# Low parts of 21 weight tiles: subtracted on GpSimd before, added up by an accumulating DMA after

## Chip, core and metric

The kernel runs on one core of a Trainium2 chip. The metric is device time in microseconds (us) of one execution. Five engines run their own instruction queues: TensorE (PE, with its weight loads PEld), VectorE (DVE), ScalarE (ACT), GpSimd (POOL) and SyncE (SP). Sixteen DMA engines move data for the queues of SP, ACT and POOL.

## What is computed

One decoder layer over 512 tokens of width 1024, in float32:

```python
h = rmsnorm(x, norm_mix[l]) * (1 + sc1) + sh1
z = h @ w_in[l]
z_attn, z_rwkv, z_conv, z_gate = split_cols(z, (ATTN_COLS, RWKV_COLS, CONV_COLS, GATE_COLS))
o_attn = dsa_attention(z_attn, positions, rel_bias)
o_rwkv = rwkv7_mix(z_rwkv, ...)
o_conv = c_b * causal_dwconv(c_c * c_x, sc_conv_w[l])
merged = sum(gates[:, :, i] * (o @ w_branch[l, i]) for i, o in enumerate((o_attn, o_rwkv, o_conv)))
x = x + g1 * (merged @ w_o[l])
x = x + g2 * conv_glu_ffn(h, ffn_w_up[l], ffn_conv_w[l], ffn_w_down[l])
```

(The second `h` is normed again, and a final norm follows.) The RWKV mix is a recurrence over time, done here in eight chunks of 64 tokens.

## The kernel before

Every large product is made of three passes, so that it has nearly float32 accuracy: each operand is split into a high part (rounded to the type fp32r) and a low part (what the rounding left), and PE adds high times high, high times low and low times high in one PSUM bank.

The projection by `w_in` goes in columns of 128 output channels. `z_col` makes one: `w_in` calls `weights`, which loads 128x1024 float32 values (512 KB, tile `wraw`, four buffers) by SP's queue, makes the high part `whi` on ACT and the low part `wlo = wraw - whi` on POOL (three buffers each); `mm_t` then issues 24 matmuls of 512 columns (eight rows k, three passes, lines L177, L178 and L179; the third reads `wlo`). The first five RWKV columns have their own buffers (`xraw`, `xhi`, `xlo`; the argument `own`) in the opening stage. The change touches the 21 columns that follow: nine of RWKV and twelve of the short convolution. After them come 18 attention columns or blocks, and later gates, branches, output projection and FFN.

The framework orders each engine's queue itself, from priorities: the weight work stands at a high priority, and the matmuls of the columns are woven between the RWKV steps on PE. An engine takes its queue strictly in order. The stages that matter here, in us of the profiled span:

- about 75 to 190: four RWKV passes (loop over `p`), each with a long row of small DVE steps (`rsqt`, `km`, `kn`, `AR`, `BK`, `r`: L243 to L505) that feed small matmuls on PE (`L486` transposes `km`, `L507` sums `r`, `L528` makes `LM`), and POOL's share (`BK` L548, `LG` L539).
- about 190 to 228: a serial substitution of 31 steps on DVE (`st` L569, `sub` L571), while PE does convolution columns.
- its result goes out to memory and back (`blk`, `Dm`); then PE multiplies by it (`L588`), and the eight chunks follow, to 310; then the RWKV tail.
- about 340 to 405: bias masks on DVE (`mk` L721) and their matmuls on PE, with attention columns and the modulation weights (`ada_w`).
- about 405 to 440: values, query and key loads, the rest of a run of `ada_w` loads.

POOL's queue also issues small loads: `g_up` (L413) and `up` (L447, L448), which the first RWKV pass multiplies by at L464.

Of the kernel before, what the change touches and what calls it, by code (L numbers as in the profile page):

```python
# [15 lines left out]
AF = mybir.ActivationFunctionType  # L16
ALU = mybir.AluOpType
# [42 lines left out]
def hybrid_block(ctx, tc, ins, out, consts, dbg=None, stop=99):  # L60
    nc = tc.nc
    PE, ACT, DVE, POOL, SP = nc.tensor, nc.scalar, nc.vector, nc.gpsimd, nc.sync
# [7 lines left out]
    def dram(name, offset, ap):  # L70
        t = ins[name]
        return bass.AP(tensor=t.tensor, offset=t.offset + offset, ap=ap)
# [10 lines left out]
    def right_pool(name):  # L83
        es = ExitStack()
        es.pool = es.enter_context(tc.tile_pool(name=name, bufs=1, side="right", reuse_waits="tile"))
        return es

    def left_pool(name):
        es = ctx.enter_context(ExitStack())
        es.pool = es.enter_context(tc.tile_pool(name=name, bufs=1, reuse_waits="tile"))  # L90
        return es
# [41 lines left out]
        return colv[tag][:, r + i:r + i + n]  # L133


    lo_engine = [POOL]

    wp = left_pool("wp")
    n_raw = 4
# [1 line left out]
    def load_raw(shape, srcs, own=None):  # L141
        if own is None:
            raw = wp.pool.tile(shape, F32, name="wraw", tag="wraw", bufs=n_raw)
        else:
            raw = own[0].tile(shape, F32, name="xraw", tag="xraw", bufs=own[1])
        for dst, ap in srcs:
            SP.dma_start(dst(raw), ap)
        return raw

    def weights(name, base, ld, k0, kt, cols, own=None, raw_own=None):  # L150


        wid = sum(n for _, n in cols)
        srcs, o = [], 0
        for c, n in cols:
            srcs.append(((lambda r, o=o, n=n: r[:, :, o:o + n]),
                         dram(name, base + k0 * 128 * ld + c, [[ld, 128], [128 * ld, kt], [1, n]])))
            o += n
        raw = load_raw([128, kt, wid], srcs, raw_own)
        pool, tag, bufs = (wp.pool, "w", 3) if own is None else (own[0], "x", own[1])  # L160
        with tc.high_priority(offset=4000):
            hi = pool.tile([128, kt, wid], F32R, name=tag + "hi", tag=tag + "hi", bufs=bufs)
            ACT.activation(hi, raw, AF.Copy)  # L163
            lo = pool.tile([128, kt, wid], F32R, name=tag + "lo", tag=tag + "lo", bufs=bufs)
            lo_engine[0].tensor_tensor(lo, raw, hi, op=ALU.subtract)  # L165
        return hi, lo

    def w_in(c0, n=128, k0=0, kt=8):
        return weights("w_in", 0, C_GATE + 3 * D, k0, kt, [(c0, n)])
# [148 lines left out]
    def first_columns(step):  # L318
        if step < len(first_cols):
            w_first[step] = weights("w_in", 0, C_GATE + 3 * D, 0, 8, [(C_RWKV + first_cols[step] * 128, 128)],  # L320
                                    own=(start.pool, len(first_cols)), raw_own=(start.pool, 8))
        for k in range(step + 1):
            for j in range(min(step + 1, len(first_cols))):
                if max(k, j) != step:
                    continue
                (hi, lo), ps = w_first[j], z_first[first_cols[j]]
                PE.matmul(ps, hi[:, k, :], hT[0][:, k, :], start=k == 0, stop=False)
                PE.matmul(ps, hi[:, k, :], hT[1][:, k, :], start=False, stop=False)
                PE.matmul(ps, lo[:, k, :], hT[0][:, k, :], start=False, stop=k == 7)
# [127 lines left out]
    for p in range(4):  # L457
# [52 lines left out]
        for w0 in range(0, 9, 4):  # L510
# [7 lines left out]
            lo = 1 if w0 == 0 else 0  # L518
# [184 lines left out]
    tap("o_conv", o_cv)  # L703


    adp = left_pool("adp")
    bi = right_pool("bi")

# [197 lines left out]
    def branch(i, o, first, last):  # L906
        for m2 in range(4):
            gate = []
            for m in range(2):
                ps = z_col(C_GATE + i * D + (m2 * 2 + m) * 128)  # L910
                sg = wk()
                if first:
                    ACT.activation(sg, ps, AF.Sigmoid)
                else:
                    ACT.activation(sg, ps, AF.Tanh, scale=0.5)
                for _ in range(4):
                    next(ada, None)
                gate.append(sg)
            for m in range(2):
                mm = m2 * 2 + m  # L920
                w = weights("w_branch", i * MIX * D, D, 0, 4, [(mm * 128, 128)])
                ps = mm_bank()
                mm_t(ps, w, o)
                dst = merged[:, mm, :]
                if first:
                    ACT.activation(dst, ps, AF.Copy, scale=2.0)
                    POOL.tensor_tensor(dst, dst, gate[m], op=ALU.mult)
                    continue
                DVE.scalar_tensor_tensor(gate[m], gate[m], 1.0, ps, op0=ALU.add, op1=ALU.mult)
                DVE.tensor_tensor(dst, dst, gate[m], op=ALU.add)  # L930
                if last:
                    ACT.activation(mg_hl[0][:, mm, :], dst, AF.Copy, scale=0.5)
                    DVE.scalar_tensor_tensor(mg_hl[1][:, mm, :], dst, 0.5, mg_hl[0][:, mm, :], op0=ALU.mult, op1=ALU.subtract)
# [387 lines left out]
```

## Time and profile before

| | us |
|---|---|
| median of 3 runs | 1178.88 |
| lowest to highest of these | 1178.0 to 1181.76 |
| the profiled execution | 1178.41 |
| its span on the core | 1176.7 |
| PE busy | 1068.0 (91%) |
| DVE busy | 744.2 (63%) |
| ACT busy | 447.3 (38%) |
| POOL busy | 366.2 (31%) |

Shares are means over stages of different limits; PE's busy time is that of pipelined matmuls, each of which is listed longer than the step from one to the next. The kernel's stages are read one by one below.

### The profile page before, as it was taken

The numbers are of one execution on the slowest core, as the hardware profiler recorded it, in microseconds if no ns is written. First come the engines' busy times: TensorE is split into PE (matmuls) and PEld (weight loads), VectorE is DVE, ScalarE is ACT, GpSimd is POOL, SyncE is SP. The second block draws the span as 40 slices with busy tenths as digits, with TensorE's granted clock in tenths as the row PEclk, the third lists the DMA queues.
The fourth block names the chain that finished last, engine by engine and source line by source line (L and its number), as shares of the span: only waits on it lengthen the run. The fifth ranks groups of instructions, "written<-read, shape, count | busy, mean of one in ns | idle before, by whom it ended". The sixth has DMA issues, their size and how long they took to land.

```text
span 1176.7 us, 17739 instructions
## 1 busy us (share of the span) xinstructions
PE 1068.0 (91%) x6822; PEld 878.9 (75%) x6822; DVE 744.2 (63%) x1331; ACT 447.3 (38%) x765; POOL 366.2 (31%) x258
## 2 busy tenths in 40 slices
PE   4889899799989989977889999997999999899996
PEld 4667677577757877765667888886988888888885
DVE  5888776833578929996445343488766676762326
ACT  4253333132334424323445333465544344442313
POOL 4233233322212344546565200015345446100001
PEclk9899999999989989989899999999999999999999
DMA  9641123231345993469975533622322332562201
GB/s 328 188 108 41 42 58 94 80 75 37 117 126 145 288 259 117 122 187 240 219 194 139 154 86 103 178 88 74 108 78 67 108 103 77 164 215 104 90 1 72
DMA packets 191649, 149.31 MB, mean 127 GB/s; under 512 B 18211, under 2 KB 167101, under 8 KB 191565
## 3 DMA queue, kind: packets, MB, share of 16 engines
q1 hardware_dynamic: 162605, 122.57, 36.2%
q0 software_dynamic: 5904, 11.08, 4.5%
q10 hardware_dynamic: 23056, 14.53, 4.2%
q8 instruction: 53, 0.87, 0.3%
q14 instruction: 31, 0.25, 0.1%
HBM read 129.53 MB, written 18.63 MB: 126 GB/s over the span
## 4 chain that ended last, share of the span: by engine, by line
PE 51%; DVE 23%; DMA 11%; issue 8%; POOL 4%; ACT 3%; SPq 0%; ACTq 0%; POOLq 0%; DVEq 0%
PE mm L179 6%; PE mm L177 6%; PE mm L178 6%; DMA xraw<-in_ada_w 3%; DMA wraw<-in_ffn_w_up 3%; DMA bt<-bias_d 2%; DVE acc L217 2%; PE sd L1245 2%; PE sd L1246 2%; PE sd L1247 2%; PE sd L177 2%; PE sd L178 2%; PE sd L179 2%; DVE sub L571 2%; DVE wlo L1012 1%
## 5 line engine op out<-in xcount | busy, mean ns | idle before, releaser
L165 POOL TENSOR_TENSOR wlo<-wraw,whi 128x1024 fp32r<-128x1024 f32 (+1 forms) x70 | 157.5, 2253 | 274.7 <-ACT whi L163 217.2
L177 PE MATMUL mm<-h_hi,whi 128*128 128x512 f32 (+2 forms) x496 | 199.9, 404 | 1.1 <-DVE o_cv L702 0.7
L178 PE MATMUL mm<-h_lo,whi 128*128 128x512 f32 (+2 forms) x496 | 199.3, 402 | 1.6 <-DVE h_lo L1071 1.5
L179 PE MATMUL mm<-h_hi,wlo 128*128 128x512 f32 (+2 forms) x496 | 199.6, 403 | 0.0
L163 ACT ACTIVATE whi<-wraw 128x1024 fp32r<-128x1024 f32 (+1 forms) x86 | 80.1, 934 | 224.2 <-PE mm L178 94.0
L178 PEld LDWEIGHTS mm<-h_lo,whi 128*128 128x128 f32 (+1 forms) x496 | 94.5, 191 | 21.5 <-DVE h_lo L1071 2.0
L177 PEld LDWEIGHTS mm<-h_hi,whi 128*128 128x128 f32 (+1 forms) x496 | 94.3, 191 | 20.7 <-issue 1.4
L179 PEld LDWEIGHTS mm<-h_hi,wlo 128*128 128x128 f32 (+1 forms) x496 | 94.7, 191 | 19.4 <-issue 0.2
L1012 DVE TENSOR_TENSOR wlo<-wraw,whi 128x1024 fp32r<-128x1024 f32 x46 | 64.9, 1410 | 61.7 <-ACT whi L1011 60.9
L1011 ACT ACTIVATE whi<-wraw 128x1024 fp32r<-128x1024 f32 x46 | 48.6, 1057 | 78.9 <-DMA wraw<-in_ffn_w_up 28.7
L217 DVE SCALAR_TENSOR_TENSOR acc<-xraw,ccol,acc 128x512 f32<-128x512 f32 x56 | 59.4, 1060 | 29.4 <-DMA xraw<-in_ada_w 28.8
L1029 POOL TENSOR_TENSOR fS<-wraw 128x512 f32<-128x512 f32 x13 | 19.5, 1500 | 182.0 <-DVE wk L986 108.0
L1042 PE MATMUL sd<-mg_hi,shi 128*128 128x256 f32 x156 | 44.9, 288 | 8.6 <-DVE p L1185 8.6
L1012 DVE TENSOR_TENSOR slo<-wraw,shi 128x1024 fp32r<-128x1024 f32 x28 | 35.5, 1266 | 21.2 <-ACT shi L1011 21.0
L1288 POOL TENSOR_TENSOR f<-f 128x512 f32<-128x512 f32 x4 | 5.7, 1414 | 135.0 <-ACT wk L988 135.0
L721 DVE TENSOR_SCALAR mk<-posq,thr 128x512 f16<-128x512 f32 (+3 forms) x128 | 45.6, 428 | 3.2 <-PE sd L727 3.2
L177 PE MATMUL mm<-o,whi 128*128 128x512 f32 x96 | 39.9, 415 | 6.2 <-DVE modc L203 6.2
L1044 PE MATMUL sd<-mg_hi,slo 128*128 128x256 f32 x156 | 44.3, 284 | 0.0
L178 PE MATMUL sd<-h_lo,whi 128*128 128x512 f32 x112 | 44.3, 395 | 0.0
L177 PE MATMUL sd<-h_hi,whi 128*128 128x512 f32 x112 | 44.2, 395 | 0.0
L179 PE MATMUL sd<-h_hi,wlo 128*128 128x512 f32 x112 | 44.2, 395 | 0.0
L1043 PE MATMUL sd<-mg_lo,shi 128*128 128x256 f32 x156 | 44.2, 283 | 0.0
(522 smaller groups left out, 2776.4 us busy)
## 6 DMA issues: line engine op xcount, KB each, us to landing
wraw<-in_w_in SPq DMA_DIRECT2D x61, 512.0 KB, 4.2
xraw<-in_ada_w SPq DMA_DIRECT2D x96, 256.0 KB, 3.9
wraw<-in_ffn_w_up SPq DMA_DIRECT2D x44, 512.0 KB, 4.3
wraw<-in_ffn_w_down SPq DMA_DIRECT2D x22, 512.0 KB, 3.4
wraw<-in_w_branch SPq DMA_DIRECT2D x24, 256.0 KB, 3.6
bias_d<-stage ACTq DMA_DIRECT2D x10, 512.0 KB, 4.9
wraw<-in_w_o SPq DMA_DIRECT2D x8, 512.0 KB, 3.8
z_att<-wk ACTq DMA_DIRECT2D x12, 256.0 KB, 2.2
```

The lines of the kernel that those rows point to most:

```text
L163: ACT.activation(hi, raw, AF.Copy)
L165: lo_engine[0].tensor_tensor(lo, raw, hi, op=ALU.subtract)
L177: PE.matmul(ps, hi[:, k, :], ahi[:, k0 + k, :], start=start and k == 0, stop=False)
L178: PE.matmul(ps, hi[:, k, :], alo[:, k0 + k, :], start=False, stop=False)
L179: PE.matmul(ps, lo[:, k, :], ahi[:, k0 + k, :], start=False, stop=stop and k == kt - 1)
L217: DVE.scalar_tensor_tensor(acc, raw, ck, acc, op0=ALU.mult, op1=ALU.add)
L721: DVE.tensor_scalar(m_[:, :n], posq[:, b * 128:], thr[:, b, gg:gg + 1], None, op0=ALU.is_ge)
L1011: ACT.activation(hi, src, AF.Copy)
L1012: DVE.tensor_tensor(lo, src, hi, op=ALU.subtract)
L1042: PE.matmul(ps, w[0][:, k], b[0][:, k], start=first and k == 0, stop=False, skip_group_check=True)
L1043: PE.matmul(ps, w[0][:, k], b[1][:, k], start=False, stop=False, skip_group_check=True)
L1044: PE.matmul(ps, w[1][:, k], b[0][:, k], start=False, stop=k == 3, skip_group_check=True)
```

## The change

For the 21 columns after the opening stage and before the attention columns, ACT writes the negated high part into `wlo`, and a DMA on POOL's queue adds `wraw` to it in place. POOL no longer subtracts there. All other weight tiles are made as before. The title given to the change also names 128-row query-key passes; these (`two_pass`) stand in the kernel before already, and the diff does not touch them.

```diff
-    lo_engine = [POOL]
+    lo_engine, lo_by_dma = [POOL], [True]
...
             hi = pool.tile([128, kt, wid], F32R, name=tag + "hi", tag=tag + "hi", bufs=bufs)
             ACT.activation(hi, raw, AF.Copy)
             lo = pool.tile([128, kt, wid], F32R, name=tag + "lo", tag=tag + "lo", bufs=bufs)
-            lo_engine[0].tensor_tensor(lo, raw, hi, op=ALU.subtract)
+            if lo_by_dma[0] and own is None:
+                ACT.activation(lo, hi, AF.Copy, scale=-1.0)
+                POOL.dma_start(lo, raw, accum_op=ALU.add)
+            else:
+                lo_engine[0].tensor_tensor(lo, raw, hi, op=ALU.subtract)
...
     tap("o_conv", o_cv)
 
 
+    lo_by_dma[0] = False
     adp = left_pool("adp")
```

POOL's queue from the opening stage into the first two RWKV passes, before:

```order
L165 TENSOR_TENSOR xlo<-xraw,xhi 128x1024 x5
L165 TENSOR_TENSOR wlo<-wraw,whi 128x1024 x3
L413 DMA g_up<-in_rwkv_g_up 128x512
L447 DMA up<-in_rwkv_w_up 64x512
L448 DMA up<-in_rwkv_a_up 64x512
L165 TENSOR_TENSOR wlo<-wraw,whi 128x1024 x2
L548 TENSOR_TENSOR BK<-BK,pc 128x512
L539 COPY LG<-LM 32x256 x2
```

And the same place after (line numbers are four or so higher):

```order
L169 TENSOR_TENSOR xlo<-xraw,xhi 128x1024 x5
L167 DMA wlo<-wraw 128x1024 x3
L417 DMA g_up<-in_rwkv_g_up 128x512
L451 DMA up<-in_rwkv_w_up 64x512
L452 DMA up<-in_rwkv_a_up 64x512
L167 DMA wlo<-wraw 128x1024 x2
L552 TENSOR_TENSOR BK<-BK,pc 128x512
L543 COPY LG<-LM 32x256 x2
```

Each subtraction became a DMA issue at the same place, and the loads of `g_up` and `up` stand behind three of them.

ACT's queue at the first RWKV pass, before:

```order
L473 ACTIVATE iP<-cs 128x512
L163 ACTIVATE whi<-wraw 128x1024
L423 ACTIVATE r<-mm,rcol 128x512
L423 ACTIVATE k<-mm,rcol 128x512
L472 ACTIVATE P<-cs 128x512
L163 ACTIVATE whi<-wraw 128x1024
L473 ACTIVATE iP<-cs 128x512
```

And after:

```order
L477 ACTIVATE iP<-cs 128x512
L163 ACTIVATE whi<-wraw 128x1024
L427 ACTIVATE r<-mm,rcol 128x512
L166 ACTIVATE wlo<-whi 128x1024
L427 ACTIVATE k<-mm,rcol 128x512
L476 ACTIVATE P<-cs 128x512
L163 ACTIVATE whi<-wraw 128x1024
L166 ACTIVATE wlo<-whi 128x1024
L477 ACTIVATE iP<-cs 128x512
```

The new copies stand right behind the high parts or one instruction later, ahead of `k` and `iP`, which feed DVE.

PE's queue where the substitution's result is used (62 of 64 small matmuls by `Dm`), before:

```order
L179 MATMUL mm<-h_hi,wlo 128x512
L177 MATMUL mm<-h_hi,whi 128x512
L588 MATMUL sd<-Dm,LG 32x32 x62
L178 MATMUL mm<-h_lo,whi 128x512
L179 MATMUL mm<-h_hi,wlo 128x512
```

And after:

```order
L181 MATMUL mm<-h_hi,whi 128x512
L182 MATMUL mm<-h_lo,whi 128x512
L592 MATMUL sd<-Dm,LG 32x32 x62
L183 MATMUL mm<-h_hi,wlo 128x512
L181 MATMUL mm<-h_hi,whi 128x512
```

Counted from the start, 520 column matmuls stand ahead of these 62 before and 533 after; ahead of the two by `Dm` that come first it is 488 and 492, and ahead of the RWKV tail's transposes (`MV`, L669) 695 and 710. So the chunks and the tail stand later in PE's order by 13 to 15 column matmuls, and as many fewer are left for the mask stage.

## Rows read from the trace of the kernel before

**Rows 1.** Tile `wlo` from 187 to 252: count, ns min/median/max, first and last start.

```profile
L165 POOL TENSOR_TENSOR wlo<-wraw,whi x10: 2352/2406/2623, 187.8 to 251.2; 128x1024 fp32r<-128x1024 f32 x10
```

**Rows 2.** Windows: stretch, length; PE, PEld, DVE, ACT, POOL busy us; clock, DMA share, GB/s.

```profile
75.00:190.00 115.00, 101.75 (x633) 78.84 (x634) 83.65 (x168) 42.11 (x74) 31.95 (x22) 0.96 0.23 57
190.00:228.00 38.00, 37.26 (x161) 29.66 (x160) 34.20 (x62) 7.03 (x8) 12.69 (x6) 1.00 0.32 86
228.00:250.00 22.00, 14.68 (x172) 11.38 (x170) 7.66 (x14) 4.83 (x6) 8.82 (x4) 0.84 0.52 120
...
340.00:405.00 65.00, 62.66 (x808) 46.60 (x807) 60.43 (x151) 28.39 (x57) 19.76 (x8) 0.97 0.68 202
405.00:440.00 35.00, 29.36 (x214) 27.86 (x213) 10.87 (x12) 7.26 (x11) 14.87 (x15) 0.90 1.06 283
```

**Rows 3.** What PE waited for from 75 to 250: us in total, times, longest.

```profile
PE sd L588 <- DMA Dm<-blk: 7.3, 1, 7.3
PE sd L486 <- DVE km L483: 5.9, 4, 3.5
PE sd L507 <- DVE r L505: 5.8, 4, 2.5
PE sd L464 <- DMA up<-in_rwkv_w_up: 1.0, 1, 1.0
```

**Rows 4.** Timeline of POOL: start us, duration us, instruction, idle before.

```profile
69.69 0.55 POOL L447 DMA_DIRECT2D up<-in_rwkv_w_up  x1
...
82.18 2.34 POOL L165 TENSOR_TENSOR wlo<-wraw,whi 128x1024 fp32r<-128x1024 f32 x1 [11.41 <-ACT whi L163]
...
198.93 2.47 POOL L165 TENSOR_TENSOR wlo<-wraw,whi 128x1024 fp32r<-128x1024 f32 x1 [3.15 <-ACT whi L163]
```

**Rows 5.** Timeline of DVE: the same instructions beside POOL's subtraction and away from it.

```profile
69.91 0.17 DVE L391 TENSOR_TENSOR rbd<-rbd,rb 128x8 f32<-128x8 f32 x1
...
82.19 2.36 DVE L245 SCALAR_TENSOR_TENSOR rsqy<-rsqt,rsqy 128x8 f32<-128x8 f32 x1
...
84.98 0.17 DVE L245 SCALAR_TENSOR_TENSOR rsqy<-rsqt,rsqy 128x8 f32<-128x8 f32 x1
...
198.48 0.30 DVE L571 TENSOR_TENSOR sub<-sub,st 128x135 f32<-128x135 f32 x1
...
199.18 2.40 DVE L571 TENSOR_TENSOR sub<-sub,st 128x156 f32<-128x156 f32 x1
...
220.76 2.89 DVE L691 SCALAR_TENSOR_TENSOR wk<-wk,cw 128x510 f32<-128x510 f32 x1
```

**Rows 6.** Timeline of PE: first use of a `wlo`, and around the wait for `Dm`.

```profile
70.94 0.40 PE L179 MATMUL mm<-h_hi,wlo 128*128 128x512 f32 x1
...
236.09 0.39 PE L588 MATMUL sd<-Dm,LG 32*32 32x32 f32 x4 [7.32 <-DMA Dm<-blk]
...
237.43 0.63 PE L178 MATMUL mm<-h_lo,whi 128*128 128x512 f32 x1
237.85 0.63 PE L179 MATMUL mm<-h_hi,wlo 128*128 128x512 f32 x1
```

**Rows 7.** Timeline of ACT: the high parts of the first three columns, and of two convolution columns.

```profile
59.62 2.94 ACT L163 ACTIVATE whi<-wraw 128x1024 fp32r<-128x1024 f32 x3
...
192.20 1.06 ACT L163 ACTIVATE whi<-wraw 128x1024 fp32r<-128x1024 f32 x1 [3.08 <-PE mm L178]
...
197.79 1.06 ACT L163 ACTIVATE whi<-wraw 128x1024 fp32r<-128x1024 f32 x1 [3.90 <-PE mm L178]
```

**Rows 8.** DMA issues: transfer, queue, count, KB each, median us from issue to landing.

```profile
x<-in_x POOLq DMA_DIRECT2D x4, 512.0 KB, 5.7
...
qi<-z_att POOLq DMA_DIRECT2D x8, 192.0 KB, 10.5
...
g_up<-in_rwkv_g_up POOLq DMA_DIRECT2D x1, 256.0 KB, 5.1
...
up<-in_rwkv_w_up POOLq DMA_DIRECT2D x1, 128.0 KB, 6.0
```

## The prediction, made before the changed kernel ran

> **What bounds the kernel now.** I read the windows first, since the mean of 91% hides the stages. From 75 to 190 us, the four RWKV passes, PE is busy 101.75 of 115 us, so 13.25 us idle; from 190 to 228 it is busy 37.26 of 38; from 228 to 250 only 14.68 of 22, at a granted clock of 0.84 [rows 2]. The reader is to see that PE has time to give back in two places alone here, and both lie in the stretch that the change touches. Next I asked who ends these waits. In the passes it is DVE: 5.9 us before the transposes of `km` and 5.8 us before the sums of `r`; at 236 it is one wait of 7.3 us for `Dm`, the result of DVE's substitution [rows 3].
>
> Then I read why DVE is late. A step of 128x8 elements takes 0.17 us at 84.98, and 2.36 us at 82.19; POOL's `wlo` began at 82.18 and ran 2.34 us [rows 4, 5]. In the substitution a step takes 0.30 us at 198.48 and the next size 2.40 us at 199.18, where POOL's `wlo` had begun at 198.93 and ran 2.47 us [rows 4, 5]. So a DVE instruction with two inputs in SBUF stands still for as long as POOL subtracts. I count seven such DVE rows from 82 to 175 (the first is that at 82.19), with an excess over the undisturbed row of 13.8 us in sum, and five from 193 to 221 (the last is that at 220.76), with 10.5 us. That POOL takes 2.4 us for one [rows 1] is not in itself what hurts: it is busy 31.95 of the passes' 115 us [rows 2].
>
> **Removed: 21 subtractions on POOL.** Their own time is on no path. What returns is DVE's 13.8 + 10.5 us, and PE gets of it only what it waited.
>
> In the passes PE waited 11.7 us for `km` and `r` [rows 3]. PE's order weaves column matmuls between the steps, and some of the lost DVE time is already covered by them, so I take two thirds, 8 us. Bounds: 4 us (half of the locks cost PE nothing) and 11.7.
>
> In the substitution all five locks lie on DVE's one chain, with DVE busy 34.2 of 38 us [rows 2], so `Dm` comes some 10 us sooner. PE stands ready at 228.8 (236.09 less 7.32 [rows 6]) and has four column matmuls more ahead of its first `Dm` matmul in the new order, which is under 1 us. The wait of 7.3 us goes. Behind it the column matmuls and the chunks are PE's own work in its own order, so I see no wait that takes its place. After the wait PE ran at half clock: matmuls follow each other at 0.42 us (237.43 to 237.85 [rows 6]), where a column of 24 takes 5.59 us (192.20 to 197.79, the cadence of ACT's `whi`, which PE releases [rows 7]), 0.233 us each. Nine matmuls ran so, up to 240.4: 9 x 0.19 = 1.7 us. Gap: 9.0 us. Bounds: 7.3 to 9.0, if PE is fed.
>
> **Added: 21 copies on ACT.** The nearest row is `whi`, the same shape, 1.06 us [rows 7]. Nine fall in the passes, where ACT is busy 42.11 of 115 us [rows 2], and some stand ahead of `k` and `iP`, which DVE waits for. If each met the path with that share of 0.37 and half its length, it would be 9 x 1.06 x 0.37 / 2 = 1.8 us; I take 2. Bounds: 0 and 5 (half of 9.5). In the substitution ACT is busy 7.03 of 38 us: nothing.
>
> **Added: 21 accumulating DMAs.** No row shows one. Call the time from issue to landing T. POOL issues a software-queue DMA in 0.55 us [rows 4], a fifth of the subtraction, so `BK` and `LG` behind it are not later. T's nearest rows are the loads of that queue: 5.7 us for 512 KB in 128 rows, 5.1 for 256 KB [rows 8]. The added DMA reads two streams of 512 KB and writes one. 256 KB more cost 0.6 us there, so I add 1.2 us for the second stream and take T = 6.9. Bounds: 5.7, and 10.5 from `qi` [rows 8], which ran while the DMA engines were fully taken (the last window of [rows 2]).
>
> What hides T: three buffers. A buffer is free when its column ends; two other columns, 2 x 5.6 us, and two matmuls, 0.5 us, pass before PE needs the new low part: 11.7 us. High part and copy take 2 x 1.14 us (a `whi` starts at 197.79 and its `wlo` at 198.93 [rows 4, 7]). So T up to 9.4 us costs nothing where columns follow each other without a break, which is from 187 to 251: nine columns of the changed kind (the tenth of [rows 1] is the first attention column). Above that every microsecond of T costs one for each three columns, 3.0 us per us. At T = 10.5 that is 3.3 us. In the passes a column comes about every 12 us (nine from 82 to 187), and T may be near 20. The four `wraw` buffers are held longer too, but four columns without a break last 22.4 us, so they bind later than the three.
>
> The Trainium skill speaks against such a queue. Its page "SBUF — State Buffer", section "SBUF: two separate sides", warns that a DMA issued from GpSimd needs its descriptors written through a port that it shares with VectorE, so that a VectorE instruction of the two-port kind starves it. The rows speak against a large effect: `up` was issued in 0.55 us while DVE worked, and a DVE step with two inputs beside that issue took its usual 0.17 us [rows 4, 5]. By the rule T grows by one such DVE step at most, some 0.5 us (an estimate); at my T the sum stays, at the upper bound it is 1.5 us worse.
>
> **Moved.** At the start, `g_up` and `up` stand behind three DMAs instead of three subtractions. The third `wlo` can be issued when ACT has done six copies, 59.62 + 6 x 0.98 = 65.5 (three took 2.94 [rows 7]), so `up` goes at about 66.8 instead of 69.69, and lands by 73 to 76 with three transfers ahead of it; PE waited 1.0 us for it [rows 3]. Gain 1.0, bounds +1.0 and -4 (T of 10.5, one behind the other). The first low part is issued at about 61.8 and needed at 70.94 [rows 6], which allows T = 9.1. On PE the RWKV tail comes 15 column matmuls later, 3.5 us. The mask stage behind it is nearly full on DVE, 60.43 of 65 us, as well as on PE, 62.66 [rows 2], so that DVE cannot make up for a late start: 3.5 us lost. Bounds: 0 and 5.
>
> **Sum.** 8.0 - 2.0 + 9.0 + 1.0 - 3.5 = 12.5 us. The profiled execution took 1178.41 us (its span 1176.7 and 1.7 around it), 0.5 us under the median of the runs, so 1178.4 - 12.5 = 1165.9 us. With all the best bounds it is 11.7 + 9.0 + 1.0 = 21.7, 1156.7 us; with the worst 4 - 5 + 7.3 - 4 - 5 - 3.3 = -6.0, 1184.4 us.
>
> **Rivals.**
> The transfer is slow, and the kernel slower. If T is above 9.4 us, PE waits on `wlo` in the nine dense columns; at T = 9.4 + 12.5/3.0 = 13.6 the gain is gone, and from 14.8 the kernel is slower by more than 0.3%. At T = 16 it is 12.5 - 19.8 = -7.3, 1185.7 us. For it: nothing in the trace shows an addition in the DMA path. Against it: no software-queue load took above 10.5 us, and that among full DMA engines; between 190 and 228 the DMA share is 0.32.
>
> The gain is given back from 340 to 440. The masks are DVE work beside POOL's subtractions that remain, and from 405 to 440 the DMA engines are full (share 1.06 [rows 2]); a new order of loads there could wait longer. Price: the 5.6 us that PE stands idle in that last window once more, plus up to 7 us of new locks on the mask row, which together take it all: 1178 us. For it: both stages are tight. Against: nothing in them starts at a fixed time; they move forward with what is ahead of them.
>
> The DMA issue holds DVE as the subtraction did, for its 0.55 us: a quarter of the 24.3 us stays, so about a quarter of 17.0 (8.0 and 9.0): 1170 us. The row at 69.91 [rows 5] speaks against it.
>
> All of PE's waits go, and ACT's copies hide: 1159 us.
>
> **How the numbers follow.** The forecast as summed has a chance of 0.58, with a range of its own of 1160 to 1172. All waits gone: 0.06. Issue holds DVE: 0.04. All three are faster, 0.68. Slow transfer: 0.18, of which 0.14 slower and 0.04 within. Given back: 0.14, of which 0.09 within and 0.05 slower. What a measurement of this kernel can tell from no change is about 0.3%, 3.5 us. So faster 0.68, same 0.13, slower 0.19. The range runs from just under the best bounds, 1155, to 1182, which leaves out the slow transfer beyond T = 14.8 or so.
>
> **What would show it.** Right: no DVE step above 1.4 us between 76 and 225, `Dm` at PE before PE is there, no wait on `L588`, clock near 1.00 from 228 to 250, and idle PE from 75 to 190 of about 5 us. Low parts landing 6 to 8 us after issue, and no wait of a column matmul on `wlo`. Wrong: PE waiting on `wlo` every third column, `up` landing after 76, ACT's copies ahead of a DVE wait, or the stage from 340 on longer than before by what the first 310 us gained.

## The result, and the profile after

The kernel got faster: 1164.56 us as the median of four runs (1163.68 to 1167.6) against 1178.44 (1177.5 to 1181.76), a ratio of 0.9872, with a 95% interval of 0.9842 to 0.9903. Repeated in a later set it was 1164.39 against 1179.36, 0.9869 (0.984 to 0.9898). The forecast was 1165.9, a gain of 12.5 us; measured were 13.9 and 15.0.

The place to look is PE's time by landmarks of the kernel rather than by fixed windows, since everything behind the first won microsecond is shifted. I cut both profiles at the last `h_lo` of the opening, the first matmul by `up`, the last transposes of `BK`, the first matmul by `Dm`, the last matmul of the eight chunks (`S`, `AR`), and the last transposes of `MV`. The five stretches between them are start, passes, gap, chunks and RWKV tail. The windows of PE after the change; a row has the stretch, its length, PE's busy time with its instructions, the granted clock, the DMA share and GB/s:

```profile
63.90:81.70 17.80, 14.34 (x62) 1.00 0.90 185
81.70:175.90 94.20, 92.93 (x610) 0.98 0.53 116
175.90:219.70 43.80, 43.80 (x190) 1.00 0.80 176
219.70:293.40 73.70, 73.53 (x885) 1.00 0.41 95
293.40:322.20 28.80, 25.20 (x212) 0.94 0.47 138
```

The same stretches of the kernel before, from a second profile of it, whose opening ended at 64.1 us as that of the changed kernel did at 63.9 (in the first it was 60.5; more on that below):

```profile
64.10:79.60 15.50, 14.41 (x63) 1.00 0.52 130
79.60:185.60 106.00, 93.09 (x610) 0.98 0.22 56
185.60:236.90 51.30, 43.23 (x187) 0.96 0.34 91
236.90:311.40 74.50, 74.01 (x875) 0.96 0.24 62
311.40:336.90 25.50, 23.29 (x207) 1.00 0.41 121
```

PE's instructions are nearly the same in each stretch, but it stands idle 12.9 us in the passes before and 1.3 after, 8.1 in the gap before and 0.0 after. At the start it stands idle 1.1 before and 3.5 after; in the tail 2.2 and 3.6. The waits of PE from 60 to 440 us after the change (in total, times, longest) say the same:

```profile
PE mm L192 <- ACT whi L163: 4.6, 1, 4.6
PE sd L673 <- DVE MV L667: 3.6, 1, 3.6
PE sd L468 <- DMA up<-in_rwkv_w_up: 3.5, 1, 3.5
PE sd L732 <- DVE mk L726: 3.0, 1, 3.0
PE mm L193 <- POOL wlo L169: 1.8, 1, 1.8
PE sd L490 <- DVE km L487: 0.8, 3, 0.4
```

Against [rows 3], the waits for `Dm` and for `r` are gone, `km` fell from 5.9 to 0.8 us, and `up` rose from 1.0 to 3.5. No matmul of a column waits for a low part that the DMA made. The waits for `whi` (L192) and `mk` lie behind the tail; the kernel before has them too, with 3.8 and 2.3 us. What the DMA costs, from the issue rows (KB each, median us to landing) and GpSimd's and DVE's timelines:

```profile
wlo<-wraw POOLq DMA_DIRECT2D x21, 512.0 KB, 5.3
```

```profile
186.22 0.85 POOL L167 DMA_DIRECT2D wlo<-wraw  x1 [4.94 <-ACT wlo L166]
```

```profile
186.50 0.24 DVE L575 TENSOR_TENSOR sub<-sub,st 128x87 f32<-128x87 f32 x1
```

T is 5.3 us in the median (4.5 to 10.1) where I took 6.9, and GpSimd spends 0.85 us on an issue where I took 0.55. The `sub` step that runs beside that issue takes 0.24 us; no DVE row from 76 to 225 us is above 1.4 us.

### The profile page after: what moved, and what is told of

It reads as the page before. It is cut to its first block, busy times and chain, and to the rows that moved or that the text cites. A ratio compares the mean times of both kernels' runs of the same rounds, so it can differ in the third digit from the quotient of the medians.

```text
span 1162.9 us, 17779 instructions
## 1 busy us (share of the span) xinstructions
PE 1067.9 (92%) x6822; PEld 878.3 (76%) x6822; DVE 717.7 (62%) x1331; ACT 467.7 (40%) x786; POOL 333.0 (29%) x258
## 4 chain that ended last, share of the span: by engine, by line
PE 60%; DVE 17%; DMA 10%; issue 7%; POOL 3%; ACT 2%; SPq 0%; ACTq 0%; DVEq 0%; POOLq 0%
PE mm L183 8%; PE mm L181 8%; PE mm L182 8%; DMA xraw<-in_ada_w 4%; DMA wraw<-in_ffn_w_up 3%; DVE acc L275 2%; DVE acc L221 2%; PE sd L181 2%; PE sd L182 2%; PE sd L183 2%; DMA bt<-bias_d 2%; PE sd L1250 2%; PE sd L1251 2%; PE sd L1252 2%; PE sd L732 1%
## 5 line engine op out<-in xcount | busy, mean ns | idle before, releaser
L169 POOL TENSOR_TENSOR wlo<-wraw,whi 128x1024 fp32r<-128x1024 f32 (+2 forms) x49 | 107.0, 2186 | 167.1 <-ACT whi L163 147.8
L221 DVE SCALAR_TENSOR_TENSOR acc<-xraw,ccol,acc 128x512 f32<-128x512 f32 x56 | 62.5, 1116 | 31.5 <-DMA xraw<-in_ada_w 31.2
L1016 ACT ACTIVATE whi<-wraw 128x1024 fp32r<-128x1024 f32 x46 | 48.6, 1057 | 80.7 <-DMA wraw<-in_ffn_w_up 28.6
L167 POOL DMA_DIRECT2D wlo<-wraw x21 | 18.2, 867 | 114.4 <-ACT wlo L166 109.1
L1017 DVE TENSOR_TENSOR slo<-wraw,shi 128x1024 fp32r<-128x1024 f32 x28 | 34.9, 1246 | 21.5 <-ACT shi L1016 21.5
```

The lines of the kernel that those rows point to most:

```text
L221: DVE.scalar_tensor_tensor(acc, raw, ck, acc, op0=ALU.mult, op1=ALU.add)
L1016: ACT.activation(hi, src, AF.Copy)
L1017: DVE.tensor_tensor(lo, src, hi, op=ALU.subtract)
```

## The experiments

All run on the chip, each against the kernel before on the same chip. Single executions of one kernel spread over 12 to 14 us there (before: 1170.37 to 1183.14 in the second set). A part of that goes with the granted clock: of the 26 executions of before in the first set, the eight shortest have a mean of 0.965, the eight longest 0.960. So I read the mechanism from the stretches and the waits and use the medians for the sign.

**Copies and order of the change, subtraction back.**

```diff
                 ACT.activation(lo, hi, AF.Copy, scale=-1.0)
-                POOL.dma_start(lo, raw, accum_op=ALU.add)
+                POOL.tensor_tensor(lo, raw, hi, op=ALU.subtract)
```

> The 21 ACT copies of the change stay, but the low part is then written over by GpSimd's subtraction, as before, and no DMA adds anything. PE, DVE and ACT have the order of the changed kernel, row for row; only GpSimd's 21 rows differ. Theory (GpSimd's subtraction makes DVE stand still, and the order is worth nothing by itself): nearly the whole gain is gone, 1176 to 1181 us, DVE steps of about 2.4 us are back between 76 and 225 us, and PE waits again before the sums and transposes of the passes and for Dm. Rival (the gain comes from the new order of PE's and ACT's queues): about 1165 us. Against the kernel before it also prices the copies: my term was a loss of 2 us, so 1180 us; if the copies hide, 1176 to 1179 us.

Measured: 1182.28 us against 1180.6, ratio 1.002 (0.9994 to 1.0046), just above the expected range. The whole gain is gone. PE's passes and gap, and its waits:

```profile
79.50:185.70 106.20, 93.09 (x610) 0.98 0.20 50
185.70:237.40 51.70, 44.18 (x190) 0.99 0.33 88
```

```profile
PE sd L511 <- DVE r L509: 10.6, 4, 3.8
PE sd L592 <- DMA Dm<-blk: 6.7, 1, 6.7
```

106.2 and 51.7 us are the values of before (106.0 and 51.3) with the order of after. DVE's locked steps are back: first one of GpSimd's subtractions, then the `sub` step inside it, the `st` step behind it, which runs alone, and a `sub` step of 175 elements beside another subtraction:

```profile
195.84 2.85 POOL L167 TENSOR_TENSOR wlo<-wraw,whi 128x1024 fp32r<-128x1024 f32 x1 [3.28 <-ACT wlo L166]
```

```profile
196.34 2.45 DVE L575 TENSOR_TENSOR sub<-sub,st 128x87 f32<-128x87 f32 x1
198.82 0.27 DVE L573 TENSOR_TENSOR st<-sub 128x112 f32<-128x112 f32 x1
201.19 2.42 DVE L575 TENSOR_TENSOR sub<-sub,st 128x175 f32<-128x175 f32 x1
```

So order and copies together bring nothing. They cost 0.2% or 2.4 us of the whole, with an interval from -0.7 to 5.4 us, and nothing in the passes, 106.2 against 106.0.

**GpSimd busy, without reading.**

```diff
+            lo = pool.tile([128, kt, wid], F32R, name=tag + "lo", tag=tag + "lo", bufs=bufs); _ = lo_by_dma[0] and own is None and [POOL.memset(lo.bitcast(F32), 0.0) for _ in range(2)]
             hi = pool.tile([128, kt, wid], F32R, name=tag + "hi", tag=tag + "hi", bufs=bufs)
             ACT.activation(hi, raw, AF.Copy)
-            lo = pool.tile([128, kt, wid], F32R, name=tag + "lo", tag=tag + "lo", bufs=bufs)
```

> The changed kernel, with two memsets of the low part on GpSimd ahead of each of the 21 copies: GpSimd is as busy as before (about 1.9 us a tile), but reads nothing. Theory (it is reading two inputs that holds DVE, not GpSimd's time): 1163 to 1168 us, and no DVE step above 1.4 us beside a memset. Rival 1 (what was won is room in GpSimd's queue, for BK, LG and the loads behind the subtractions): 1173 to 1179 us with DVE undisturbed. Rival 2 (any GpSimd work on SBUF holds DVE): 1173 to 1179 us with DVE steps of 1 to 2 us beside the memsets.

Measured: 1167.7 us, ratio 0.9901 (0.9867 to 0.9935), and no DVE row above 1.45 us from 76 to 232. PE's passes and gap:

```profile
82.10:177.60 95.50, 92.77 (x611) 0.98 0.52 112
177.60:222.30 44.70, 43.88 (x191) 1.00 0.80 176
```

They are 1.3 and 0.9 us longer than the changed kernel's, not 12 and 8. A pair of memsets, and two of DVE's steps that lie in it:

```profile
190.74 1.97 POOL L162 MEMSET wlo<- 128x1024 f32 x2 [1.40 <-PE mm L183]
```

```profile
190.82 0.34 DVE L575 TENSOR_TENSOR sub<-sub,st 128x175 f32<-128x175 f32 x1
191.67 0.35 DVE L573 TENSOR_TENSOR st<-sub 128x192 f32<-128x192 f32 x1
```

The step on 175 elements took 2.42 us beside a subtraction in the kernel with the subtraction back, and 0.34 here. GpSimd's time (1.97 us a pair, against 2.4 for a subtraction) is not what hurt: what it did in that time is. The Trainium skill has a rule for steps with two inputs: its page "SBUF — State Buffer", section "SBUF: two separate sides", has a VectorE operation with two SBUF inputs contend only with a GpSimd operation that reads SBUF. The subtraction reads two tiles, the memset none, and for these steps the two runs agree with it; whether a GpSimd operation that reads a single tile holds them, no run shows.

The memsets are not harmless to every DVE step, though. Six copies and scalar operations with one input tile were lengthened beside them from 88 to 161 us, by 3.0 us in sum. Two of the six, of which each takes 0.17 us in the changed kernel:

```profile
88.77 0.75 DVE L478 COPY pc<-P 128x8 f32<-128x8 f32 x1
160.71 1.00 DVE L496 TENSOR_SCALAR AR<-kn 128x8 f32<-128x8 f32 x1
```

So the second rival, that any GpSimd work on SBUF holds DVE, is right for such steps and wrong for those with two inputs, which carry the loss: the median stayed under its 1173 to 1179 us.

**One stage each.** The DMA for the nine RWKV columns alone, then for the twelve convolution columns alone:

```diff
+    lo_by_dma[0] = False
     for m in range(4):
         ps_c = z_col(C_CONV + 512 + m * 128)
```

> The accumulating DMA makes only the nine RWKV low parts; the twelve of the convolution are subtracted on GpSimd. Three of those twelve fall into the passes, nine beside the substitution and behind it. Theory (each stretch wins what its own locks cost): two thirds of the passes' 14.7 us stay, the Dm wait is back: 1178.4 - 9.8 + 2.4 = about 1171 us (1168 to 1174). Rival (only the substitution's gain reaches the end, as what the passes win is waited out at Dm): 1176 to 1179 us.

```diff
-    lo_engine, lo_by_dma = [POOL], [True]
+    lo_engine, lo_by_dma = [POOL], [False]
...
+    lo_by_dma[0] = True
     for m in range(4):
         ps_c = z_col(C_CONV + 512 + m * 128)
```

> The other way round: only the twelve convolution low parts come from the DMA, the nine of RWKV from GpSimd's subtraction. Theory: the Dm wait is gone (7.5 us) and a third of the passes' 14.7 us is won (4.9 us), the RWKV tail loses 1.7 us, the loads of up are on time again: 1178.4 - 10.7 = about 1168 us (1165 to 1171), and the gains of this kernel and of the one with RWKV alone add up to the whole, 14 us, within 3 us. Rival (the passes carry the gain): 1174 to 1179 us.

Measured: RWKV alone 1169.87 us, 0.9897 (0.9857 to 0.9937); convolution alone 1174.35 us, 0.9943 (0.9915 to 0.997), both against 1180.6. Start, passes and gap of RWKV alone, then passes and gap of the other:

```profile
59.90:77.70 17.80, 14.39 (x62) 0.98 0.90 185
77.70:174.80 97.10, 95.18 (x611) 0.95 0.43 96
174.80:225.90 51.10, 43.20 (x188) 0.98 0.34 91
```

```profile
80.00:184.80 104.80, 93.50 (x610) 0.98 0.31 71
184.80:228.70 43.90, 43.90 (x191) 1.00 0.80 177
```

Each stretch wins on its own and keeps it. RWKV alone brings the passes to 97.1 us (108.9 in the first profile of before, whose opening ended as early) and leaves the gap at 51.1; convolution alone brings the gap to 43.9 and takes 1.2 us off the passes. The gains, 10.7 and 6.3 us, add up to 17.0 where the whole was expected to be 14 and is 14 to 15, just within the 3 us allowed. My split of the passes by number of columns was off: the three convolution columns in them are worth about 1 us, not 4.9, and that puts convolution alone 3 us above its range. The rival, that the passes' gain is waited out at `Dm`, is wrong.

**Two buffers in place of three.**

```diff
-        pool, tag, bufs = (wp.pool, "w", 3) if own is None else (own[0], "x", own[1])
+        pool, tag, bufs = (wp.pool, "w", 2) if own is None else (own[0], "x", own[1])
...
-        pool, tag, bufs = (wp.pool, "w", 3) if ring is None else (fs.pool,) + ring
+        pool, tag, bufs = (wp.pool, "w", 2) if ring is None else (fs.pool,) + ring
```

> The changed kernel with two buffers instead of three for the high and low parts of these tiles and of the later ones from the same place. My sum had three buffers hide a landing time up to 9.4 us. With two, one other column and two matmuls (6.1 us) lie between the end of a column and the need of the next low part in its buffer; high part, copy and transfer take 2.3 + 5.3 = 7.6 us. Theory: PE waits about 1.5 us for wlo at every second column of the dense stretch from 185 to 240 us, some 6 us in all, and that stretch is longer by as much. Rival (the weave leaves more room than that): waits on wlo under 2 us in sum. The whole time says less, as later stages lose a buffer too: 1172 to 1200 us.

Measured, one run: 1178.42 us. From 180 to 240 us PE waits for low parts, and the transfers land in:

```profile
PE mm L183 <- DMA wlo<-wraw: 10.7, 5, 2.7
```

```profile
wlo<-wraw POOLq DMA_DIRECT2D x8, 512.0 KB, 5.9
```

Five waits on nine columns, every second one, as the count of buffers has it, and 2.1 us each: high part and copy 2.3, landing 5.9, less 6.1 us that cover them. The expected 6 us had the landing at 5.3. So the third buffer is what hides this DMA, and the arithmetic by which 9.4 us are free with three holds with two.

**The start.** `up` came later than before, and stood behind three accumulating transfers on GpSimd's queue. First its two loads on another queue, then the first three low parts subtracted on GpSimd again:

```diff
-    POOL.dma_start(up[0:64], dram("rwkv_w_up", 0, [[512, 64], [1, 512]]))
-    POOL.dma_start(up[64:128], dram("rwkv_a_up", 0, [[512, 64], [1, 512]]))
+    SP.dma_start(up[0:64], dram("rwkv_w_up", 0, [[512, 64], [1, 512]]))
+    SP.dma_start(up[64:128], dram("rwkv_a_up", 0, [[512, 64], [1, 512]]))
```

> The changed kernel with the two loads of up issued by SyncE instead of GpSimd, so that they don't stand behind three accumulating transfers in one queue. Theory (they landed 8.5 us after their issue, and PE waited 3.5 us): they land 2 to 4 us after issue, PE's wait at line 468 goes to under 1 us, and the kernel is 2 to 4 us faster than the changed one, 1160.5 to 1162.5 us if that is 1164.6. Rival 1 (the loads are late because their tile's memory comes free late, not because of the queue): no change, 1164 to 1166 us. Rival 2 (SyncE stands still at them and the weight loads behind are late): 1166 to 1169 us, with PE waiting for high parts.

```diff
-    lo_engine, lo_by_dma = [POOL], [True]
+    lo_engine, lo_by_dma, n_col = [POOL], [True], [True] * 18 + [False] * 3
...
-            if lo_by_dma[0] and own is None:
+            if lo_by_dma[0] and own is None and n_col.pop():
```

> The changed kernel, but the first three of the 21 low parts, which are made while the first pass's loads are on their way, are subtracted on GpSimd as before. Theory (from 66 to 84 us the DMA engines are full, with a share above 1.0, since three transfers more came into that stretch, and that is why up lands 8.5 us after its issue, by whatever queue): without the three, up lands 6 to 6.6 us after its issue, the first matmul by it starts about 15.5 us behind the last h_lo instead of 17.9, and the kernel is 2 to 3 us faster than the changed one, about 1162 us where that is 1164.4. Rival (these three subtractions stop DVE in the opening's end, as before, and that costs as much as the transfers): no difference, 1163.5 to 1166 us.

Measured: on SyncE 1167.05 us, 0.9893 (0.9868 to 0.9919), beside 0.9869 of the changed kernel in the same set: no gain, so the theory is wrong, and PE's wait for `up` grew to 7.2 us. The time lies in the second rival's range, but its sign, new waits of PE for high parts, is not in the trace. With three subtractions 1158.64 us, 0.9808 (0.9779 to 0.9838). The issue rows of `up` on SyncE (duration), PE's start there, and PE's start and passes with three subtractions:

```profile
L451 SPq DMA_DIRECT2D up<-in_rwkv_w_up x1: 3604/3604/3604, 72.4 to 72.4; - x1
L452 SPq DMA_DIRECT2D up<-in_rwkv_a_up x1: 1722/1722/1722, 76.1 to 76.1; - x1
```

```profile
61.40:82.90 21.50, 14.35 (x63) 0.92 0.90 196
```

```profile
63.70:79.10 15.40, 14.43 (x63) 1.00 0.52 130
79.10:172.50 93.40, 91.75 (x610) 1.00 0.53 114
```

On SyncE the start grew from 17.8 to 21.5 us: the issue itself took 3.6 us for the first load and 1.7 for the second. In the windows of the changed kernel the share of the DMA engines (last column but one) shows why another queue did not help there:

```profile
64.00:68.00 4.00, 4.00 (x18) 3.21 (x18) 2.65 (x16) 3.94 (x5) 1.41 (x2) 1.00 0.33 60
68.00:72.00 4.00, 4.00 (x18) 3.20 (x17) 1.08 (x8) 1.21 (x2) 1.22 (x2) 1.00 1.03 179
72.00:76.00 4.00, 4.00 (x19) 3.22 (x18) 3.02 (x12) 3.31 (x5) 1.65 (x3) 1.00 1.08 227
76.00:80.00 4.00, 2.24 (x10) 1.48 (x8) 0.54 (x3) 2.10 (x4) 0.00 (x0) 1.00 1.08 271
80.00:84.00 4.00, 2.30 (x6) 1.36 (x7) 0.12 (x1) 0.84 (x2) 0.00 (x0) 0.79 1.19 252
```

From 68 to 84 us they are full: three accumulating transfers, four raw tiles, `g_up` and `up` all at once. Without the three, the start is 15.4 us as before, and the last `MV` comes 3.3 us sooner behind the opening's end (255.0 against 258.3 us). The medians, of two different sets, lie 5.8 us apart, and the gains over each set's own kernel before, 22.8 and 15.0, 7.9. By any of these the expected 2 to 3 us was low.

**Copies and addition priced.** A plain DMA of the raw tile into the low part, and no copy on ACT:

```diff
-                ACT.activation(lo, hi, AF.Copy, scale=-1.0)
-                POOL.dma_start(lo, raw, accum_op=ALU.add)
+                POOL.dma_start(lo, raw)
```

> The changed kernel without the copies on ACT, and with a plain DMA of the raw tile into the low part in place of the accumulating one. (So the high part is not taken off: the low parts hold the whole weight.) It prices copies and addition together. Theory (both are hidden except at the start): the transfers land in 4.0 to 4.8 us instead of 5.3, up lands a little sooner, and the kernel takes 1161 to 1164.5 us where the changed one takes 1164.4. Rival (ACT's copies stand ahead of evictions that DVE waits for, my term of 2 us and its bound of 5): 1159 to 1161.5 us, with the passes from the first matmul by up to the last transpose of BK shorter by 2 to 5 us.

Measured: 1152.52 us, 0.9757 (0.9729 to 0.9785), faster than theory and rival had it. Start, passes and gap:

```profile
63.00:78.00 15.00, 14.36 (x63) 1.00 0.69 177
78.00:171.60 93.60, 90.93 (x611) 1.00 0.37 107
171.60:214.50 42.90, 42.90 (x187) 1.00 0.66 192
```

The passes take 93.6 us, as with the copies and three subtractions (93.4), so the rival's place is wrong: ACT's copies cost nothing there. The transfers landed in 3.0 us (median of the 21) where I had expected 4.0 to 4.8.

But this kernel differs from the changed one by more than copies and addition, so it does not price them. Without the copies, the order on PE, DVE and ACT is that of the kernel before, instruction for instruction from the first matmul by `up` on. And a plain transfer needs no high part: the first three went out at 53.6 to 54.7 us, ahead of the opening's end, and so left the start. Up to the last `MV` this kernel is 8.0 us shorter than the changed one (2.8 at the start, 0.6 in the passes, 0.9 in the gap, 1.9 in the chunks, 1.8 in the tail), where gap, chunks and tail hold 15 column matmuls fewer; 2.5 us of that are lost again behind it.

The profiled executions, counted from the opening's end, lie 5.5 us apart (1156.5 - 63.0 against 1162.9 - 63.9), the medians 12. The rest comes from which execution was profiled: that one took 1158.54 us at a granted clock of 0.965, the other five 1150.1 to 1153.15 at 0.971 or 0.972. Why their clock is higher no run shows. Beside the kernel before, whose order it has, it shows what goes with the subtractions: passes of 93.6 us instead of 106.0 and a gap of 42.9 instead of 51.3.

**Attention columns too**, and both edits together:

```diff
-    lo_by_dma[0] = False
     adp = left_pool("adp")
...
+    lo_by_dma[0] = False
     for c in range(0, 512, 256):
         w = [w_in(C_ATT + 2 * MIX + c, 256, k0, 4) for k0 in (0, 4)]
```

> The accumulating DMA goes on through the attention columns up to the values (twelve whole tiles and one of 72 columns more). Theory (what a lock costs is what waits behind it): only two or three DVE steps between 230 and 395 us stood still beside a subtraction, with about 5 us of excess, of which PE's waits for MV (3.6 us) and mk (3.0 us) can give back 2 to 4 us; copies on ACT cost 0 to 1.5 us: 1161 to 1165 us. Rival (copies on ACT and transfers stand in the way of the masks' evictions, the modulation loads and the query loads from 340 to 440 us): 1166 to 1172 us.

> The best of both: the first three low parts on GpSimd, the other eighteen and those of the attention columns by the accumulating DMA. If the two edits add up: 1159.2 - 2.5, about 1156.5 us (1154.5 to 1159). If the first three make no difference: 1158.5 to 1160.5 us.

Measured: 1159.24 us, 0.9825 (0.9797 to 0.9853), 5.2 us under the changed kernel in the same set and more than the 2 to 4 expected; together with the first three on GpSimd 1155.11 us, 0.9782 (0.9751 to 0.9813), within the range expected if the two edits add up. Of the kernels that leave nothing out that is the fastest, 26.4 us under before. PE's chunks and tail in it:

```profile
216.80:298.50 81.70, 79.37 (x889) 0.92 0.51 115
298.50:321.90 23.40, 23.40 (x208) 1.00 0.72 174
```

PE's waits for `MV` (3.6 us) and `mk` (3.0) are gone. The chunks are 8.0 us longer than the changed kernel's (at a granted clock of 0.92 instead of 1.00) and the tail 5.4 shorter, and the last `MV` comes no sooner than there (321.9 against 322.2, with three subtractions alone 318.7); the gain appears behind it, with the masks. New waits are small (`ki` 2.6, `TT` 1.2).

**The kernel before, a second profile.**

> The kernel before once more, for its opening and for the stages behind 440 us. If where the opening ends is chance, the last h_lo ends anywhere between 59.5 and 64.5 us (60.5 in the first profile); if the change moved it, at 60 to 61 us again. From the first matmul by up to the last transpose of BK it takes 107 to 110 us, and PE waits 6.5 to 7.5 us for Dm, as in the first profile.

Measured: 1180.31 us, its opening ending at 64.1, passes 106.0 (a microsecond under the expected 107 to 110; the granted clock was 0.98 in them, 0.95 in the first profile) and a wait of 7.3 us for `Dm`. In the first profile, with the opening ending at 60.5, the five stretches were 15.4, 108.9, 51.3, 73.7 and 27.1 us. And the changed kernel again:

> The changed kernel itself once more, as the base of its neighbours, and for the opening stage, which ended 3.4 us later in its profile than before though its order is the same on every engine. Theory (that is chance: where the opening's subtractions on GpSimd fall against DVE's steps): about 1165 us, and the last h_lo ends anywhere between 60 and 64.5 us. Rival (the change moves the opening, through the first transfers): it ends at 63.5 to 64.5 us again.

Its opening ended at 59.8 us, and its stretches were 17.9, 96.2, 43.9, 73.6 and 28.7 us. So where the opening ends is chance, in either kernel.

## Why the prediction was right, step by step

Two pairs of profiles have openings that end alike: at 60 us (the first profile of before, second of after) and at 64 us (the other two). Gains in us, from the opening's end:

| stretch | predicted | pair at 60 | pair at 64 |
|---|---|---|---|
| start (`up`) | 1.0 | -2.5 | -2.3 |
| passes (waits less copies) | 6.0 | 12.7 | 11.8 |
| gap at `Dm`, chunks | 9.0 | 7.5 | 8.3 |
| RWKV tail | -3.5 | -1.6 | -3.3 |
| behind it | 0 | 2.4 | 1.0 |
| sum | 12.5 | 18.5 | 15.5 |

**The mechanism is shown.** DVE stands still while GpSimd subtracts; with the subtraction back, in the same order on PE, DVE and ACT, the gain is gone, and with GpSimd nearly as busy but reading nothing most of it stays (12.9 us, where the change won 13.9 and 15.0). That the sum of 12.5 us came so near is in part luck: the passes won about 6 us more than forecast, and the start came some 3.4 us under its term. Of the signs named beforehand, PE's idle time from 75 to 190 us (4.7 us for the expected 5) and a clock of 1.00 from 228 to 250 came true, a landing of 6 to 8 us did not. One word of the working was too narrow: besides steps with two inputs in SBUF, the scalar operation `km<-a,rcol`, with one input tile, took 2.28 us beside a subtraction where it takes 0.54 alone:

```profile
113.39 2.28 DVE L492 TENSOR_SCALAR km<-a,rcol 128x512 f32<-128x512 f32 x1
```

**Passes: a term mis-sized.** I gave PE two thirds of its 11.7 us back, since column matmuls would cover some locks. They covered none that mattered: idle time fell from 12.4 and 12.9 us to 0.9 and 1.3, which is the upper bound of the term. The 2.0 us for ACT's copies did not show in the passes in either comparison (106.2 against 106.0, and 93.4 against 93.6 without them).

**Gap and tail: a term in the wrong place.** The 7.3 us of wait went, and nothing took its place; the half clock is gone too (clock 1.00 in the chunks after, 0.96 and 0.97 before). The two stretches won 7.5 and 8.3 us although they took in 14 column matmuls more, which PE had done later before (lines L177 to L179 count 47, 46 and 47 matmuls in the chunks before, the same lines of the changed kernel 50, 50 and 50, and four more lie in the gap). At 0.233 us each these are 3.3 us. So most of the -3.5 us for the 15 matmuls was paid here, and wait and clock together gave back 10.8 and 11.6 us (an estimate from these numbers), more than the 9.0 of the term.

The tail holds one column matmul more (68 instead of 67), and grew by 1.6 and 3.3 us for other reasons: PE waits 3.6 us for `MV` instead of 2.2, and in the pair at 64 the granted clock was 0.94 instead of 1.00. That the -3.3 is close to the term of -3.5 is luck. The kernel with the subtraction back has the same tail, 28.6 us at a clock of 0.94, so it comes with the order. Behind the tail 15 column matmuls fewer are left, and 1.0 to 2.4 us come back where I had put nothing.

**Start: the step that failed.** "So `up` goes at about 66.8 instead of 69.69, and lands by 73 to 76 with three transfers ahead of it" is wrong in both halves. The loads were issued no sooner: 9.2 us behind the opening's end in the kernel before (69.69) and in both profiles of the changed one (69.02 and 73.08). In the profile with the early opening GpSimd's third `wlo` was issued at 65.47, as forecast, but `g_up` then stood 2.1 us, by the profile until a matmul of the opening's columns (L333) was done. And they landed 8.5 and 8.6 us after the issue instead of 6.0, since the DMA engines were full (without the three transfers it is 6.0 again): at 81.6 and 77.6 us, behind the 76 that the prediction itself had named as a sign of being wrong. So the term of +1.0 us measured -2.3 and -2.5. The first three tiles on GpSimd undo the loss.

**The DMA.** T of 5.3 us lay under my lower bound of 5.7, which came from loads out of DRAM by the same queue. The sum did not hang on it, since up to 9.4 us are hidden; the waits with two buffers are what the same count gives for two.

**The rivals.** A slow transfer, and a DMA issue that holds DVE, are excluded by T and by the 0.24 us step beside an issue. Giving back from 340 to 440 did not happen: the stage behind the tail gains 1 to 2.4 us. That all waits go (1159 us, for which no working is given; by the terms it is 1160) was right for the passes and the gap; it missed the start.

**Still open:** the higher granted clock of the plain DMA's other executions, what the addition alone costs, and differences of 2 to 4 us behind the first 440 us, which two profiles of one kernel have as well.

## What to carry to other kernels

When a GpSimd instruction that reads SBUF runs beside a chain of two-input DVE steps, ask what each DVE step loses and whose wait ends with it, not how busy GpSimd is; here 2.4 us of GpSimd, far off PE's path, cost a DVE step up to 2.4 us, and the 21 of them cost PE some 20 us of idle time (12.9 and 8.1 us before, 1.3 and 0.0 after). A DMA that adds in place can take over, where enough buffers cover high part, copy and landing. Leave it out where the DMA engines are full already: three of the 21 transfers gave back 3.3 us of what the others won.

## What the runs showed of the hardware that I had not expected

- An accumulating DMA of 512 KB between two SBUF tiles lands in 5.3 us in the median, quicker than the plain 512 KB load by the same queue in [rows 8] (5.7), slower than the plain transfer between the same tiles (3.0), and costs GpSimd 0.85 us to issue against 0.55.
- Two GpSimd memsets of 128x1024 (0.95 us each) beside DVE steps with two inputs cost these nothing, while a COPY and a TENSOR_SCALAR of 128x8 with one input tile took 0.75 and 1.00 us beside them instead of 0.17.
- A load of 64 rows took SyncE 3.6 us to issue while the DMA engines were full.
- The opening ended between 59.8 and 64.4 us in all fourteen profiles, in either kernel at both ends. The passes behind a late opening were shorter, by 2.9 us in the kernel before (106.0 instead of 108.9) and by 2.0 in the changed one (94.2 instead of 96.2). It is not that waits absorb it, since PE's idle time did not fall (12.9 us behind the late opening and 12.4 behind the early one, in the changed kernel 1.3 and 0.9): the granted clock was 0.98 instead of 0.95 in both, and PE's busy time shorter.
